# Cross-attention's output projection as seven block products for eight, with weight sums made in DRAM, and two idle products

## The chip, the core and the metric

The kernel runs on one core of a Trainium2 chip. That core has a matrix engine (TensorE; PE in the profile, its weight loads PEld), a vector engine (VectorE, DVE), an activation engine (ScalarE, ACT), GpSimd (POOL) and SyncE (SP), which here only issues DMAs. The metric is the device time of one execution in microseconds (us).

## The reference

One encoder layer on 512 tokens of width 1024 in float32. A state-space branch and a gated MLP branch are merged into the residual `h`; then come cross-attention to 256 memory tokens, a SwiGLU feed-forward layer and a last norm. The change is at the end of the attention, and reaches into the feed-forward layer:

```python
def memory_cross_attention(hn, memn, w_q, w_k, w_v, w_o):
    ...
    p = jax.nn.softmax(s, axis=-1).astype(v.dtype)
    o = jnp.einsum('bhlm,bmhd->blhd', p, v).reshape(bsz, seq, D_MODEL)
    return o @ w_o

def swiglu(hn, w_gate, w_up, w_down):
    return (jax.nn.silu(hn @ w_gate) * (hn @ w_up)) @ w_down
...
        h = h + memory_cross_attention(rms_norm(h, xattn_norm_g[i]), memn,
                                       w_q[i], w_k[i], w_v[i], w_xo[i])
        h = h + swiglu(rms_norm(h, ffn_norm_g[i]), w_gate[i], w_up[i], w_down[i])
```

There are 4 heads of 256; `w_xo` (the reference's `w_o`) is 1024 x 1024; the feed-forward width is 2816.

## The kernel before

**Precision.** Every large product is made of three passes. Each float32 operand is split into a rounded part and a remainder: `split` (L83) casts on ScalarE (L85) and subtracts on VectorE (L86), and `mm3` (L350; L1276 for the block products of the queries and the feed-forward units) multiplies high by high, high by low and low by high into one PSUM bank. So each piece of weights of 128 x 1024 elements a partition block costs a DMA, a cast and a subtract before TensorE may use it. The pieces are listed in a plan in the order of their use. `next_w` (L322) takes the next; it issues the load of the piece three entries ahead (some loads of the feed-forward units 4, 5 or 7 ahead) and the split of the piece two entries ahead. There are three buffers for raw pieces and three for split ones. PSUM has five banks called `mm` and three called `aux`.

**Seven for eight.** The queries (`w_q`), the gate and up weights of the feed-forward layer and `w_down` already use a scheme in which a product of 2 x 2 blocks by 2 x 2 blocks takes seven block products instead of eight, on sums of blocks. Token sums are made by VectorE. Weight sums of `w_q` and `w_down` are made in DRAM: a job copies a block to a scratch tensor by a DMA on SP's queue (L267), and a later DMA on POOL's queue adds another block to it (L268). `plan_sums` (L252) hangs these jobs at given plan entries: (entry of the copy, entries from there to the accumulate). There are 32 jobs: 8 for `w_q`, 24 for `w_down` (`qsum`, `dsum`). The units of gate and up make their weight sums with a POOL DMA and VectorE.

**The stage of the change.** The queries end at about 508 us. Then, head by head, `scores` (L1225) makes softmax probabilities, `turn_probs` transposes them on TensorE and splits them, and `values` (L1259) multiplies them by the values, into `po`, which is split at once into `ot_hi` and `ot_lo`, the transposed attention output. `w_xo` is a plain product: output columns 0 to 511 for all four token tiles by `tokm` (L1364), with the values of heads 1 to 3 called between its pieces, then columns 512 to 1023 (L1376), two token tiles at a time. Each finished bank is added to `h` (L1153), its squares are summed (L475), and when a token's row is complete `norm_feat` scales it (L501), transposes it on TensorE (`to_feat`, L509) and splits it into `fn_hi`, `fn_lo`, which the feed-forward layer reads. That layer begins with 256 leftover columns of gate and up (`pf`), and then takes ten units of 512 columns, seven block products of 24 matmuls each (`px`, `pv`, `pq`); `w_down` follows in seven products (`dx`, `dq`, `dv`), with 42 pieces.

**Order.** The program is written in one order and a scheduler, which goes by its own estimate of the times, may exchange instructions that don't depend on each other, on each engine; what is marked with `in_order` stays. `later(n, f)` puts off the writing of a step by n units of product work. In units 1 and 2 `between` (L1522) puts idle work on TensorE, kept in order, that nobody reads: 15 transposes of 128 columns (`t`, L1527) and two products of 512 columns (`p`, L1529).

## Time and profile before

| | us |
|---|---|
| median of three runs (908.34 to 910.14) | 908.49 |
| the profiled execution | 908.83 |
| its span, first instruction to last | 907.0 |
| queries, values, w_xo: last product of `w_xo` begins | 574.7 |
| feed-forward units end, only `w_down` left | 799.6 |

The page of the profile gives each engine's busy time over the span, then the chain of work that ended last, followed back from the end; its shares say where the time went. Windows give busy time by stage. A group of instructions is listed by its source line, engine, operation and tile names, with its busy time, the mean duration of one in ns, and the idle time ahead of it with what ended it. A mean duration holds a part that overlaps with the next instruction; the distance between starts of instructions that stand back to back, or a chain piece's time divided by its count, is what one more costs. In the chain, `pt` is w_xo (and other token products), `po` values, `psc` scores, `ptr` transposes after a norm.

### The profile page before, as it was taken

The numbers are of one execution on the slowest core, as the hardware profiler recorded it, in microseconds if no ns is written. First come the engines' busy times: TensorE is split into PE (matmuls) and PEld (weight loads), VectorE is DVE, ScalarE is ACT, GpSimd is POOL, SyncE is SP. The second block draws the span as 40 slices with busy tenths as digits, with TensorE's granted clock in tenths as the row PEclk, the third lists the DMA queues.
The fourth block names the chain that finished last, engine by engine and source line by source line (L and its number), as shares of the span: only waits on it lengthen the run. The fifth ranks groups of instructions, "written<-read, shape, count | busy, mean of one in ns | idle before, by whom it ended". The sixth has DMA issues, their size and how long they took to land.

```text
span 907.0 us, 14526 instructions
## 1 busy us (share of the span) xinstructions
PE 895.5 (99%) x5659; PEld 791.6 (87%) x5659; DVE 623.5 (69%) x1018; ACT 475.6 (52%) x696; POOL 104.3 (12%) x165
## 2 busy tenths in 40 slices
PE   9999999999999999999999999999999999999996
PEld 6878888888888887889999978999999999988885
DVE  5696662888753235858956836786778777799875
ACT  5543985144375244446655635655455455565664
POOL 1004320110025301011001001100011100000010
PEclk9999999999999999999999999999999999999999
DMA  7566574586546577863569416527678984246672
GB/s 238 172 161 178 125 179 138 164 201 156 141 135 153 130 198 225 279 190 119 173 221 278 138 51 186 154 58 185 163 198 222 221 198 116 70 139 198 199 234 101
DMA packets 111718, 153.80 MB, mean 170 GB/s; under 512 B 13521, under 2 KB 78561, under 8 KB 111586
## 3 DMA queue, kind: packets, MB, share of 16 engines
q1 hardware_dynamic: 92450, 127.22, 44.4%
q0 software_dynamic: 16608, 24.62, 16.7%
q10 hardware_dynamic: 2592, 1.05, 0.5%
q8 instruction: 44, 0.72, 0.3%
q14 instruction: 24, 0.20, 0.1%
HBM read 146.08 MB, written 38.24 MB: 203 GB/s over the span
## 4 chain that ended last, share of the span: by engine, by line
PE 92%; ACT 3%; DMA 2%; issue 1%; DVE 1%; POOL 0%; SPq 0%; POOLq 0%; DVEq 0%; ACTq 0%
PE pf L350 28%; PE pt L350 16%; PE px L1276 12%; PE dx L350 6%; PE pq L1276 6%; PE dq L350 3%; PE pv L1276 3%; PE qx L1276 2%; PE dv L350 2%; PE pk L789 2%; PE ptr L509 1%; PE psc L350 1%; PE qq L1276 1%; PE po L350 1%; DMA xt<-in_x_dram 1%
## 5 line engine op out<-in xcount | busy, mean ns | idle before, releaser
L86 DVE TENSOR_TENSOR wlo<-wraw,whi 128x1024 fp32r<-128x1024 f32 (+1 forms) x139 | 165.1, 1188 | 109.2 <-ACT whi L85 107.6
L85 ACT CAST whi<-wraw 128x1024 fp32r<-128x1024 f32 (+1 forms) x139 | 142.5, 1025 | 163.1 <-PE pf L350 70.5
L350 PE MATMUL pf<-xn,whi 128*128 128x512 f32 x448 | 140.0, 392 | 0.0
L350 PEld LDWEIGHTS pf<-xn,whi 128*128 128x128 f32 x448 | 83.5, 188 | 17.0 <-issue 0.2
L350 PE MATMUL pf<-xn,wlo 128*128 128x512 f32 x224 | 87.4, 390 | 0.0
L1276 PE MATMUL px<-fn,whi 128*128 128x256 f32 x480 | 84.4, 278 | 0.0
L1276 PEld LDWEIGHTS px<-fn,whi 128*128 128x128 f32 x480 | 72.8, 188 | 0.2
L85 ACT CAST whi<-b 128x1024 fp32r<-128x1024 f32 x40 | 42.2, 1054 | 54.5 <-PE px L1276 29.2
L86 DVE TENSOR_TENSOR wlo<-b,whi 128x1024 fp32r<-128x1024 f32 x40 | 48.9, 1223 | 31.4 <-ACT whi L85 31.4
L1276 PE MATMUL px<-fn,wlo 128*128 128x256 f32 x240 | 66.7, 278 | 0.0
L1276 PE MATMUL pq<-s,whi 128*128 128x256 f32 x320 | 55.7, 278 | 0.0
L350 PE MATMUL dx<-whi,s 128*128 128x512 f32 x170 | 53.6, 391 | 0.4 <-DVE h L1632 0.4
L86 DVE TENSOR_TENSOR wlo<-t,whi 128x1024 fp32r<-128x1024 f32 x30 | 36.7, 1224 | 19.9 <-ACT whi L85 19.9
L85 ACT CAST whi<-t 128x1024 fp32r<-128x1024 f32 x30 | 31.6, 1053 | 35.6 <-PE pv L1276 12.6
L350 PEld LDWEIGHTS pf<-xn,wlo 128*128 128x128 f32 x224 | 42.1, 188 | 8.7
L1276 PEld LDWEIGHTS pq<-s,whi 128*128 128x128 f32 x320 | 48.4, 188 | 0.0
L1276 PEld LDWEIGHTS px<-fn,wlo 128*128 128x128 f32 x240 | 45.2, 188 | 0.0
L1276 PE MATMUL pq<-s,wlo 128*128 128x256 f32 x160 | 44.4, 277 | 0.0
L350 PE MATMUL pt<-whi,xn 128*128 128x512 f32 x128 | 43.6, 412 | 0.1
L350 PEld LDWEIGHTS dx<-whi,s 128*128 128x128 f32 x170 | 31.8, 188 | 7.3 <-issue 0.8
L350 PE MATMUL dx<-wlo,s 128*128 128x512 f32 x85 | 33.1, 391 | 0.0
L1276 PEld LDWEIGHTS pq<-s,wlo 128*128 128x128 f32 x160 | 30.1, 188 | 0.0
(420 smaller groups left out, 2239.2 us busy)
## 6 DMA issues: line engine op xcount, KB each, us to landing
wraw<-in_w_in_dram SPq DMA_DIRECT2D x36, 512.0 KB, 4.3
dsum<-in_w_down_dram SPq DMA_DIRECT2D x20, 512.0 KB, 6.2
wraw<-dsum SPq DMA_DIRECT2D x20, 512.0 KB, 4.4
b<-in_w_gate_dram SPq DMA_DIRECT2D x15, 512.0 KB, 4.7
b<-in_w_up_dram SPq DMA_DIRECT2D x15, 512.0 KB, 4.5
wraw<-in_w_down_dram SPq DMA_DIRECT2D x15, 512.0 KB, 3.6
dsum<-in_w_down_dram POOLq DMA_DIRECT2D x10, 512.0 KB, 7.1
dsum<-dsum POOLq DMA_DIRECT2D x10, 512.0 KB, 6.6
```

The costliest lines, as they stand in the source:

```text
L85: hi = nc.scalar.copy(dst_hi, src)
L86: lo = nc.vector.tensor_tensor(dst_lo, src, dst_hi.bitcast(F32), ALU.subtract)
L350: m = nc.tensor.matmul(ps, a[x], b[y], start=start and i == 0, stop=stop and i == 2, skip_group_check=free)
L509: nc.tensor.transpose(ps[:, j, :], src[:, k * P:(k + 1) * P], ident)
L789: nc.tensor.matmul(ps[32 * j:32 * j + 32, q, :], bd[i][:, g].rearrange("p d c -> p (d c)"), lc(es[i], g), start=(i == 0), stop=False, tile ...
L1276: nc.tensor.matmul(ps[:, j, :], a[x], b[y], start=start and j == k == i == 0, stop=k == 3 and i == 2, skip_group_check=True)
```

## The change

`w_xo` becomes one 2 x 2 block product. Tokens are halved into T0 (0 to 255) and T1, its 1024 rows into K0 and K1 (heads 0 and 1, heads 2 and 3), its columns into two halves. With O the attention output and W the weights, in blocks of 512 rows and columns, the seven products are

| product | token operand | weights | added to h (tokens, columns) |
|---|---|---|---|
| 1 | O(T1,K0) | W00 | + (T1, 0); goes on into 6 |
| 7 | O(T1,K0) - O(T0,K0) | W01 + W11 | - (T0, 1); goes on into 4 |
| 6 | O(T0,K0) - O(T0,K1) - O(T1,K0) | W00 + W01 + W11 | 1 + 6: - (T0, 1), + (T0, 0), - (T1, 1) |
| 5 | O(T0,K0) - O(T0,K1) | W00 + W01 | + (T0, 1); goes on into 3 |
| 4 | O(T0,K1) | W00 + W01 + W11 + W10 | 7 + 4: + (T0, 0) |
| 2 | O(T1,K1) | W10 | + (T1, 0) |
| 3 | O(T1,K1) + operand of 6 | W11 | 5 + 3: + (T1, 1) |

Each has two pieces of weights (c = 0, 1; 12 matmuls of 512 columns each), 14 for eight before. The four weight sums are made in DRAM by eight jobs, put between those of `w_q` and those of `w_down`; the jobs' places in the plan are given anew, so that eight more of the `w_down` jobs come in the feed-forward units. `values` no longer splits `po`; it copies it to `of`, and `attention_part` makes the operands: products 1 and 7 from heads 0 and 1 alone, the others when heads 2 and 3 are there. The first pieces of 1 and 7 stand between the values of heads 1, 2 and 3. Operands 5 and 6 lie in two tiles of the attention's pool. The norms of T0 are begun after product 4, those of T1 after product 3, which is done token tile by token tile. The idle work in units 1 and 2 goes; there are two idle products of 512 columns instead, one after the second product of unit 0 and one after its product 5 (`between()`), reading `fn_hi[:, 4, :]`, where those before read `fn_hi[:, 0, :]`.

```diff
--- before.py
+++ after.py
@@ -220,6 +220,28 @@
 
             plan.append(((w_q, 512 * n, q), [(LOADS, load)], lambda got=got: halves(got.pop("raw"))))
 
+    XSRC = {1: (0, 0), 2: (1, 0), 3: (1, 1)}
+    xsum = {q: dp.tile([P, KD // 2, 512], F32, name=f"xsum{q}") for q in (4, 5, 6, 7)}
+    XO = ((1, 0), (7, 0), (1, 1), (7, 1), (6, 0), (5, 0), (6, 1), (5, 1), (4, 0), (4, 1), (2, 0), (2, 1), (3, 0), (3, 1))
+
+    def xo_block(i, j, c):
+        return block(w_xo, 4 * i + 2 * c, 2, 512 * j, 512)
+
+    def xo_sum(q, c):
+        return xsum[q][:, 2 * c:2 * c + 2, :]
+
+    def plan_xo():
+        for q, c in XO:
+            got = {}
+
+            def load(q=q, c=c, got=got):
+                got["raw"] = wp.tile([P, 2, 512], F32, tag="raw", name="wraw", bufs=3)
+                nc.sync.dma_start(got["raw"], xo_block(*XSRC[q], c) if q in XSRC else xo_sum(q, c))
+
+            plan.append(((w_xo, q, c), [(LOADS, load)], lambda got=got: halves(got.pop("raw"))))
+
     def plan_units(units, down):
 
@@ -258,6 +280,10 @@
             for n in range(2):
                 jobs.append((qsum[q, n], qsum[q + (-1 if q == 6 else 2), n] if first is None else query_block(*first, n),
                              more(n)))
+        for q, first, more in ((5, (0, 0), lambda c: xo_block(0, 1, c)), (7, (0, 1), lambda c: xo_block(1, 1, c)),
+                               (6, (1, 1), lambda c: xo_sum(5, c)), (4, (1, 0), lambda c: xo_sum(6, c))):
+            for c in range(2):
+                jobs.append((xo_sum(q, c), xo_block(*first, c), more(c)))
         for q, i, jc, more in ((5, 0, 0, lambda c: down_block(0, 1, c)), (7, 0, 1, lambda c: down_block(1, 1, c)),
                                (6, 1, 1, lambda c: down_sum(5, c)), (4, 1, 0, lambda c: down_sum(6, c))):
             for c in range(CHUNKS):
@@ -306,9 +332,7 @@
     for half in range(2):
         plan_tok(w_v, half * 512, KD)
     plan_queries()
-    plan_tok(w_xo, 0, KD)
-    for i in range(4):
-        plan_block(w_xo, 2 * i, 2, 512, 512, place=(None, None, 2, 4)[i])
+    plan_xo()
     FS = 2560
     UNITS = [(w, c0) for c0 in range(0, FS, 512) for w in (w_gate, w_up)]
     down_tokens, down_plan = [], []
@@ -316,7 +340,7 @@
     plan_units(UNITS, down_plan)
 
     plan_sums([(5 + 3 * i, 3) for i in range(12)] + [(40 + 2 * i, 2) for i in range(8)] +
-              [(79 + 3 * i, 3) for i in range(3)] + [(116 + 5 * i, 4) for i in range(9)])
+              [(79 + 3 * i, 3) for i in range(3)] + [(122 + 4 * i, 3) for i in range(17)])
     used_w = [0]
 
     def next_w(*key):
@@ -1262,7 +1286,8 @@
             cs = slice(hd * XD + dt_ * P, hd * XD + dt_ * P + P)
             for mt in range(NM):
                 mm3(ps, (vts[0][:, mt, cs], vts[1][:, mt, cs]), (p_hi[:, mt, :], p_lo[:, mt, :]), mt == 0, mt == NM - 1)
-            split(ot_hi[:, 2 * hd + dt_, :], ot_lo[:, 2 * hd + dt_, :], ps)
+            nc.scalar.copy(of[:, 2 * hd + dt_, :], ps)
+        attention_part(hd)
 
     def product(ps, u, q, start, ops):
 
@@ -1342,26 +1367,82 @@
     query_part(3, T0, u2)
     ot_hi = slot("D", (P, KD, T), F32R, "ot_hi")
     ot_lo = slot("E", (P, KD, T), F32R, "ot_lo")
+
+    of = slot("B", (P, KD, T), F32, "of")
+    ot_q = lambda ks, ts: (ot_hi[:, ks, ts], ot_lo[:, ks, ts])
+    xops = {1: ot_q(K0, T1), 2: ot_q(K1, T1), 4: ot_q(K1, T0), 7: ot_q(K0, T0), 3: ot_q(K0, T1)}
+
+    def attention_part(hd):
+
+        u = slice(2 * (hd % 2), 2 * (hd % 2) + 2)
+        lw = slice(u.start + 4, u.stop + 4)
+        a11, a12, a21, a22 = (of[:, k, t] for t in (T1, T0) for k in (u, lw))
+
+        def operand(q, src):
+            split(xops[q][0][:, u], xops[q][1][:, u], src)
+
+        if hd < 2:
+            operand(1, a11)
+            s3_ = np_.tile([P, 2, 256], F32, tag="ev", name="s3", bufs=2)
+            nc.vector.tensor_tensor(s3_, a11, a21, ALU.subtract)
+            operand(7, s3_)
+            return
+        nc.vector.tensor_tensor(a21, a21, a22, ALU.subtract)
+        nc.vector.tensor_tensor(a11, a21, a11, ALU.subtract)
+        operand(6, a11)
+        operand(5, a21)
+        operand(4, a22)
+        operand(2, a12)
+        nc.vector.tensor_tensor(a12, a12, a11, ALU.add)
+        later(2, lambda: operand(3, a12))
+
+    g_f = gain(ffn_norm_g[0], "g_f")
+
+    def xo_product(ps, q, c, start, stop, w=None, ts=(0, 1)):
+        hi, lo = w or next_w(w_xo, q, c)
+        a = xops[q]
+        for t in ts:
+            tsl = slice(t * P, (t + 1) * P)
+            for k in range(2):
+                mm3(ps[t], (a[0][:, 2 * c + k, tsl], a[1][:, 2 * c + k, tsl]), (hi[:, k, :], lo[:, k, :]),
+                    start and k == 0, stop and k == 1, True)
+        tick(1.35 * len(ts))
+
+    def onto(ps, t0, half, op):
+        for t in range(2):
+            hs = h[:, t0 + t, HALF[half]]
+            nc.vector.tensor_tensor(hs, hs, ps[t], op)
+
+    def half_done(t, half):
+        sum_sq(hss[:, 1, t, half:half + 1], h[:, t, HALF[half]])
+
     values(0, *pts.pop(0))
     probs2 = scores(2)
     probs3 = scores(3)
+    for q, nm in ((5, "kt_hi"), (6, "kt_lo")):
+        s_ = ap_.tile([P, KD, M], F32R, name=nm).rearrange("p (i k) t -> p i k t", i=2)
+        xops[q] = s_[:, 0], s_[:, 1]
     turn(1, probs1)
-
-    def second():
-        values(1, *pts.pop(1))
-        turn(2, probs2)
-        turn(3, probs3)
-
-    def last_two():
-        for i in (2, 3):
-            values(i, *pts.pop(i))
-
-    g_f = gain(ffn_norm_g[0], "g_f")
-    ot = (ot_hi, ot_lo)
-    fn_hi, fn_lo = token_slot("fn", APART)
-    fn = (fn_hi, fn_lo)
-
-    tokm(w_xo, 0, ot, KD, add_evac(0, 1, None), hooks={1: second, 2: last_two})
+    ox = [bank("ox0"), bank("ox1")]
+    xo_product(ox, 1, 0, True, False)
+    values(1, *pts.pop(1))
+    turn(2, probs2)
+    oy = [bank("oy0"), aux("oy1")]
+    xo_product(oy, 7, 0, True, False)
+    values(2, *pts.pop(2))
+    turn(3, probs3)
+    xo_product(ox, 1, 1, False, True)
+    onto(ox, 2, 0, ALU.add)
+    values(3, *pts.pop(3))
+    xo_product(oy, 7, 1, False, True)
+    onto(oy, 0, 1, ALU.subtract)
+    oq = [bank("oq0"), bank("oq1")]
+    xo_product(ox, 6, 0, False, False)
+    xo_product(oq, 5, 0, True, False)
+    xo_product(ox, 6, 1, False, True)
+    onto(ox, 0, 1, ALU.subtract)
+    xo_product(oq, 5, 1, False, True)
     at.close()
     ff = ExitStack()
     fp = ff.enter_context(tc.tile_pool(name="ffn", bufs=1))
@@ -1369,24 +1450,36 @@
     sx = ExitStack()
     stp[0] = sx.enter_context(tc.tile_pool(name="units", bufs=2))
     full = fp.tile([P, KD, T], F32, tag="full", name="full", bufs=1)
-
-    fin = add_evac(1, 1, feat_norm(g_f, fn_hi, fn_lo, full))
-    held = []
-    for t0 in (0, 2):
-        ps = {t: bank(f"pt{t - t0}") for t in (t0, t0 + 1)}
-        for wi in range(2):
-            if t0 == 0:
-                held.append((wi,) + next_w(w_xo, 2 * wi, 2, 512, 512))
-            for t in ps:
-                tok_block(ps[t], t, held[wi:wi + 1], ot, 2, slice(0, 512), wi == 0, False)
-            tick(2.7)
-        if t0 == 0:
-            held += [(wi,) + next_w(w_xo, 2 * wi, 2, 512, 512) for wi in (2, 3)]
-        for t in ps:
-            tok_block(ps[t], t, held[2:4], ot, 2, slice(0, 512), False, True)
-            fin(t, ps[t])
-            tick(2.7)
+    onto(oq, 0, 1, ALU.add)
+    onto(ox, 0, 0, ALU.add)
+    for t in range(2):
+        half_done(t, 1)
+    onto(ox, 2, 1, ALU.subtract)
+    xo_product(oy, 4, 0, False, False)
+    xo_product(oy, 4, 1, False, True)
+    fn_hi, fn_lo = token_slot("fn", APART)
+    fn = (fn_hi, fn_lo)
+    to_fn = feat_norm(g_f, fn_hi, fn_lo, full)
+    for t in range(2):
+        hs = h[:, t, HALF[0]]
+        nc.vector.tensor_tensor(hs, hs, oy[t], ALU.add)
+        half_done(t, 0)
+        to_fn(t, hss[:, 1, t, :])
+    ov = [bank("ov0"), bank("ov1")]
+    xo_product(ov, 2, 0, True, False)
+    xo_product(ov, 2, 1, False, True)
+    onto(ov, 2, 0, ALU.add)
+    for t in (2, 3):
+        half_done(t, 0)
+
+    ws = [next_w(w_xo, 3, c) for c in range(2)]
+    for t in range(2):
+        for c in range(2):
+            xo_product(oq, 3, c, False, c == 1, ws[c], (t,))
+        hs = h[:, 2 + t, HALF[1]]
+        nc.vector.tensor_tensor(hs, hs, oq[t], ALU.add)
+        half_done(2 + t, 1)
+        to_fn(2 + t, hss[:, 1, 2 + t, :])
 
@@ -1461,10 +1554,15 @@
         feat_block(ps, ws[i], fn, KD, 4, ts, ts is T0)
         tick(2.7)
 
+    def between():
+
+        in_order(nc.tensor.matmul(aux("idle"), ops[1][0][:, 0, 0:P], fn_hi[:, 4, :], start=True, stop=True))
+
     gate_part(0, T0)
     begun = unit_start(UNITS[0])
     gate_part(1, T0)
     unit_second(UNITS[0], begun[1])
+    between()
     for i in range(2):
         gate_part(i, T1)
     for j in range(2):
@@ -1519,29 +1617,17 @@
             rows_product(ps, q, c, next_w(w_down, q, c), (0, 1), slice(0, 512), start and c == 0, c == CHUNKS - 1,
                          chunks[0] == c > 0)
 
-    def between(*what):
-
-        rest_ = aux("idle")
-        for w in what:
-            if w == "t":
-                in_order(nc.tensor.transpose(rest_[:, 0:P], ident, ident))
-            else:
-                in_order(nc.tensor.matmul(rest_, ops[1][0][:, 0, 0:P], fn_hi[:, 0, :], start=True, stop=True))
-
     for i, u in enumerate(UNITS):
         final = i == len(UNITS) - 1
         x, v = begun
         q = unit_bank("pq")
-        if i in (1, 2):
-            between(*"tt")
         product(q, u, 5, True, ops)
         if final:
             last_job.append(u)
             make_tokens(1, 0)
         if i == 0:
             split(*fn_q(K0, T1), s3)
-        if i in (1, 2):
-            between(*"pt"[:i])
+            between()
         product(x, u, 6, False, ops)
         u2 = stp[0].tile([P, 2, 256], F32, tag="u2", name="u2", bufs=2)
         u3 = np_.tile([P, 2, 256], F32, tag="ev", name="u3", bufs=2)
@@ -1551,8 +1637,6 @@
         else:
             dx = [bank(f"dx{t}") for t in range(2)]
             down_product(dx, 1, True, range(1))
-        if i in (1, 2):
-            between(*"tttt"[:i * 2 - 1])
         product(x, u, 7, False, ops)
         nc.scalar.copy(u3, x)
         if i == 0:
@@ -1563,8 +1647,6 @@
             down_product(dx, 1, True, range(1, 2))
         V.tensor_tensor(u3, q, u3, ALU.subtract)
         put(u, 1, T1, u3)
-        if i in (1, 2):
-            between(*("tttt", "tt")[i - 1])
         product(x, u, 4, False, ops)
         put(u, 0, T1, x)
         if u[0] is w_up:
```

## The prediction

> **What bounds the kernel now.** I read the page's busy shares first, then the chain that ended last, then that chain in order of time around the change, the busy time by stage, and the groups of the stage.

> ```profile
> span 907.0 us, 14526 instructions
> PE 895.5 (99%) x5659; PEld 791.6 (87%) x5659; DVE 623.5 (69%) x1018; ACT 475.6 (52%) x696; POOL 104.3 (12%) x165
> ...
> PE 92%; ACT 3%; DMA 2%; issue 1%; DVE 1%; POOL 0%; SPq 0%; POOLq 0%; DVEq 0%; ACTq 0%
> ```

> TensorE is the bound: 92% of the chain. A product that goes away is time won, unless something else then comes late. The chain in order of time shows what one product costs:

> ```profile
> 547.75 17.32 PE pt L350 x76
> ...
> 588.18 16.96 PE pf L350 x144
> ...
> 622.11 2.83 PE pq L1276 x24
> 624.93 0.22 PE idle L1527 x2
> 625.15 2.83 PE pq L1276 x24
> 627.98 0.23 PE idle L1529
> 628.21 5.45 PE px L1276 x48
> ...
> 648.54 0.11 PE idle L1527
> 648.64 5.66 PE px L1276 x48
> ...
> 676.85 2.72 PE pv L1276 x24
> ...
> 824.19 14.96 PE dv L350 x66
> ```

> A product of 512 columns costs 14.96/66 = 0.2267 us (the w_xo stretch: 17.32/76 = 0.228). One of 256 columns has two paces: 24 cost 2.83 us or 2.72 us, each kept over long stretches, at the same granted clock (1.00, below), and changing where idle products stand. Next, the stages (us, then busy us of PE, PEld, DVE, ACT, POOL, granted clock, DMA share, GB/s):

> ```profile
> 463.90:508.40 44.50, 44.50 (x394) 44.46 (x393) 28.92 (x42) 26.38 (x43) 2.48 (x3) 1.00 0.81 238
> 508.40:575.00 66.60, 65.66 (x331) 54.14 (x331) 40.22 (x75) 32.62 (x68) 3.02 (x4) 1.00 0.38 111
> 680.00:745.00 65.00, 65.00 (x576) 65.00 (x575) 52.37 (x53) 33.84 (x42) 9.69 (x9) 1.00 0.91 216
> 748.00:780.00 32.00, 32.00 (x285) 32.00 (x284) 24.53 (x25) 16.72 (x21) 1.34 (x1) 1.00 0.34 83
> ```

> The attention values and w_xo are the second line: VectorE is busy 60% of it, PE idle 0.94 us. The feed-forward units are the last two; while sums of w_down are made, DMA is at 0.91. The groups of the second line's window give the durations:

> ```profile
> L86 DVE TENSOR_TENSOR wlo<-wraw,whi 128x1024 fp32r<-128x1024 f32 x5 | 6.1, 1223 | 7.2 <-ACT whi L85 7.2
> L86 DVE TENSOR_TENSOR ot_lo<-po,ot_hi 128x512 fp32r<-128x512 f32 x8 | 5.4, 687 | 11.5 <-ACT ot_hi L85 11.5
> L1153 DVE TENSOR_TENSOR h<-h,pt 128x512 f32<-128x512 f32 x7 | 4.6, 681 | 1.7 <-PE pt L350 1.7
> ```

> **The change part by part.** The sum is made against the profiled execution: 908.83 us, its span of 907.0 and 1.83 around it. It lies 0.34 us (0.04%) above the median of 908.49; 0.2%, 1.8 us, is about what a measurement here can tell from no change.

> Products. Before, w_xo is 4 token tiles x 2 halves x 8 blocks of k x 3 passes = 192 products of 512 columns; after, seven of 2 x 4 x 3 = 168. 24 x 0.2267 = **-5.44 us**, on the path. [...]

> VectorE and the waits it makes in this stage. Added: 14 weight pieces for 8, +6 splits; 14 operand splits for 8, +6 subtracts of 512 columns; 8 sums of tokens; 18 additions to h for 8, +10. Back to back, the timeline has two 1024 splits in 2.36 us and three h additions in 1.88, so 1.18 and 0.63 each: 6 x 1.18 + 24 x 0.63 = 22.2 us. VectorE goes from 40.2 to 62.4 us in a stage that TensorE alone would do in 66.6 - 5.4 = 61.2. It is full. The surplus is 1.2 us. Where a pass depends on it: after each of the last two heads stands copy 0.59, two sums 1.37, cast 0.59, subtract 0.69 = 3.2 us ahead of products 6 and 5. Cover is 36 products x 0.227 = 8.2 us, if the queue ahead of it on VectorE is short. If that cover is gone for both heads, 6.4 us; if there is no new wait and the old 0.94 us goes too, -0.9. I take the surplus plus one wait as long as the longest there now (0.68): **+1.9 us**, near the low end, because VectorE's overfull time can slide past the last product: the sums for tokens 256 to 511 aren't needed until four blocks of 24 products (11 us) later.

> ACT: 6 more casts at 1.05 and 14 of 0.59 (the eight old ones become plain copies): 32.6 + 14.6 = 47 of 61 us, hidden under TensorE. Onto h: product 6 waits until product 1's bank has been added to h, 4 likewise for 7, 3 for 5; one to six pieces of 2.7 us lie between. These are priced in the 6.4. The banks held longer leave two for the transposes of the norm, as many as a tile uses: 0, and at most one 0.35 us group four times over if it does not.

> Idle products. Removed: 15 transposes and two products of 512, in the chain 0.22 + 0.23 + 0.11 + 0.44 + 0.22 + 0.23 + 0.11 + 0.33 + 0.22 = 2.11 us; added: two of 0.23. **-1.65 us**, on the path.

> Pace. Of 78 blocks of 24 products of 256 columns between 575 and 800 us, about 27 go at 2.83 now (the chain: 18 before 628, 2 at 639.7, 4 from 648.6 to 660, 3 after 788). All fast is 27 x 0.11 = -3.0; all slow (78 - 27) x 0.11 = +5.6. The one place where a lone product of 512 columns stands between slow products is 627.98: fast after it. At 648.30 a transpose follows it and the pace is slow. The new ones stand alone, after some four blocks, so I take fast from there, and keep four early and three late slow blocks: 20 x 0.11 = **-2.2 us**.

> DMAs. Eight sums (a copy of 512 KB on SP, an accumulate on POOL) take the places of eight w_down sums early on: same sizes, same places, 0. Their bounds are 0 and, if a weight piece is late by the copy's median 6.2 us once, +6.2; I take 0 since the copies stay as they are. Those eight move into the units: 17 jobs, one per 4 plan entries with 3 between copy and accumulate, for nine at 5 and 4. In the w_xo stage 14 loads come for 8, at a share of 0.38: hidden. Queues: SP issues 14 more (0.37 and 0.56 us each), POOL 8 more (0.87 each), both mostly idle; behind an accumulate that waits for its copy stands the next unit's own accumulate on POOL. Cover for that is three entries (8.2 us) against a copy that lands in 6.2. I take 0, with the upper end in rival D.

> Sum: 908.83 - 5.44 + 1.9 - 1.65 - 2.2 = **901.4 us**, 0.8% below the median.

> **The rivals.**

> B, VectorE becomes the bound: both chains exposed, +6.4 for +1.9: **905.9**. For: 62.4 of 61.2 us. Against: the last w_down stage runs at 72.43 of 84 busy on VectorE with no wait.

> C, the two idle products do not change the pace or set the slow one, and the units go at 2.83 throughout: +5.6 for -2.2: **909.2**, no change. For: at 648.30 and 785.65 slow products follow one of 512. Against: 627.98.

> E, the pace is where it was, because nothing steers it: term 0, **903.6**. [...]

> D, the other side: DMA is the bound in the units. Share 0.34 without jobs, 0.91 with about one per 13.6 us; at one per 10.9 us 0.34 + 0.57 x 1.25 = 1.05, so 5% of 50 entries x 2.72 = 136 us, +6.8; and an accumulate that lands late then holds POOL, another 3 us at each of two or three units with two accumulates in flight (they landed in 10.67 us at worst): 901.4 + 6.8 + 7.5 = **915.7**. It decides once a unit's load takes over four entries, 10.9 us; the slowest now took 9.9. Against: in the first line of the table, jobs at three entries ran beside a load per entry at 238 GB/s, and PE was busy 44.50 of 44.50. [...]

> **How the numbers follow.** Forecast 0.45 (its own range 898.5 to 904), E 0.13, B 0.14, C 0.12, D 0.11; B and C together (about 913.7) 0.05. Faster: forecast, E and B, 0.72; same: C, 0.12; slower: D and B with C, 0.16. The low end is all fast and no new wait, 901.4 - 0.8 - 2.8 = 897.8; the high end takes in C, 909.8. What lies above is 0.16, below some 0.03.

> **What the profile after would show.** Right: 168 products of 512 from w_xo; VectorE over 90% busy from the first of them to the units; the chain there on PE with at most 3 us of idle; units at 2.72 after the second idle product; no wait of a weight cast on a DMA in the units. Wrong: PE waiting for the splits of sums (B), 2.83 through the units (C), PE or ACT waiting on loads of `b` or `t` after 620 us (D).

## The result, and the profile after

Eleven runs of the changed kernel had a median of 905.3 us (903.23 to 908.48), against 909.82 for the kernel before beside them: a ratio of 0.9957, with a 95% interval of 0.9945 to 0.9969. Twelve more runs in another comparison (`e16_changed_again`) had 907.22 against 909.11: 0.9973 (0.9961 to 0.9985). So the change makes the kernel 0.3 to 0.4% faster. The forecast of 901.4 us is 0.9% under 909.82. The sign is right and 905.3 lies inside the outer range (897.8 to 909.8), but above the forecast's own range (898.5 to 904), and the gain is half the forecast or less.

The page of the changed kernel's first profiled execution (908.21 us, near the top of its runs; a second profile, of `e16_changed_again`, was taken of the fastest of its twelve, 903.84 us) begins like this; the last line is the chain's shares by engine.

```profile
span 906.4 us, 14551 instructions
PE 889.8 (98%) x5620; PEld 785.7 (87%) x5620; DVE 643.9 (71%) x1048; ACT 488.1 (54%) x716; POOL 111.0 (12%) x173
...
PE 84%; DMA 4%; ACT 4%; DVE 4%; issue 2%; POOL 0%; SPq 0%; ACTq 0%; POOLq 0%; DVEq 0%
```

TensorE's busy time fell by 5.7 us, the span by 0.6. Its share of the chain went from 92% to 84%: where it left TensorE, it now runs through VectorE, ScalarE and DMAs. The windows say where (us, then busy us of PE, PEld, DVE, ACT, POOL, granted clock of TensorE as a share of full speed, DMA share, GB/s): values and `w_xo`; the first products of the feed-forward layer; all from there to the product `dv` of `w_down`.

```profile
511.40:573.10 61.70, 59.66 (x303) 49.41 (x302) 56.16 (x96) 41.48 (x80) 2.42 (x3) 1.00 0.47 146
573.10:593.10 20.00, 18.41 (x142) 18.09 (x143) 14.32 (x23) 13.87 (x24) 2.38 (x3) 0.91 0.74 209
593.10:822.20 229.10, 229.10 (x1887) 223.66 (x1886) 183.60 (x185) 123.06 (x149) 26.11 (x25) 1.00 0.76 195
```

VectorE is busy 91% of the first window. In the second TensorE is idle for 1.6 us, and its granted clock is 0.91. In the third nothing waits. To compare kernels I cut every trace at the same places: the front (to the first product of the values), the stage (values, `w_xo`, the start of unit 0, until 120 products of the leftover columns are still to come), the units (to the first product of `dv`) and the rest. In us, with the difference to the kernel before:

| | front | stage | units | rest | span |
|---|---|---|---|---|---|
| before | 508.4 | 82.4 | 233.2 | 83.0 | 907.0 |
| predicted | 0 | -3.3 | -4.1 | 0 | -7.4 |
| changed, first profile | +3.0 | -0.8 | -4.0 | +1.2 | -0.6 |
| changed, second profile | +0.8 | -2.6 | -4.0 | +0.8 | -5.0 |
| best version, below | -0.1 | -4.9 | -3.9 | +1.6 | -7.3 |

The units came out as predicted. The stage fell short by 0.7 to 2.5 us, and the front, put at nothing, cost 0.8 or more.

TensorE's waits between 555 and 600 us in the first profile (engine, line, what it waited for: us in total, times, longest):

```profile
PE ptr L533 <- ACT full L537: 1.6, 1, 1.6
PE oq L374 <- DVE wlo L86: 1.5, 2, 1.1
PE pf L374 <- ACT fn L85: 0.6, 1, 0.6
```

None of them is a wait for the operands of products 5 and 6, where the prediction had looked. They stand at product 3 (`oq`), at the norm's transposes (`ptr`) and at the first leftover products (`pf`). The chain in order of time (start, us, what) shows what is behind them:

```profile
555.72 6.29 DMA wraw<-in_w_xo_dram
562.11 1.06 ACT whi L85
563.19 1.23 DVE wlo L86
...
564.83 0.57 POOL r L510
...
568.76 1.15 DVE wlo L86
569.93 3.72 DMA wraw<-in_w_gate_dram
573.67 1.04 ACT s L85
...
575.91 4.24 PE pf L374 x22
```

VectorE did six additions to `h` from 550.89 on, and only then the remainder of a weight piece that had been cast since 552.1. So one of the three raw buffers came free late, at 555.7; the load of product 3's first piece landed at 562.0; ScalarE's cast waited 3.3 us for it. Behind that cast stood the squares of T0's norm, and behind the subtract (563.19) VectorE's part of the norm, whose input `h` had been ready since 560.3. The same thing happens once more with a gate piece (569.93). The last line is a second cost: 22 products of 256 columns in 4.24 us, near half the pace (the granted clock was 0.50 there, see the end of the experiments).

### The profile page after: what moved, and what is told of

Its sections match the earlier page's. It is cut to its first block, busy times and chain, and to the rows that moved or that the text cites. A ratio compares the mean times of both kernels' runs of the same rounds, so it can differ in the third digit from the quotient of the medians.

```text
span 906.4 us, 14551 instructions
## 1 busy us (share of the span) xinstructions
PE 889.8 (98%) x5620; PEld 785.7 (87%) x5620; DVE 643.9 (71%) x1048; ACT 488.1 (54%) x716; POOL 111.0 (12%) x173
## 3 DMA queue, kind: packets, MB, share of 16 engines
q10 hardware_dynamic: 2592, 1.05, 0.5%
## 4 chain that ended last, share of the span: by engine, by line
PE 84%; DMA 4%; ACT 4%; DVE 4%; issue 2%; POOL 0%; SPq 0%; ACTq 0%; POOLq 0%; DVEq 0%
PE pf L374 27%; PE px L1301 12%; PE pt L374 11%; PE dx L374 6%; PE pq L1301 6%; PE pv L1301 3%; PE qx L1301 2%; PE dq L374 2%; PE pk L813 2%; PE po L374 1%; PE psc L374 1%; PE qq L1301 1%; PE ptr L533 1%; DVE wlo L86 1%; PE dv L374 1%
## 5 line engine op out<-in xcount | busy, mean ns | idle before, releaser
L86 DVE TENSOR_TENSOR wlo<-wraw,whi 128x1024 fp32r<-128x1024 f32 (+1 forms) x147 | 174.7, 1189 | 106.3 <-ACT whi L85 104.4
L85 ACT CAST whi<-wraw 128x1024 fp32r<-128x1024 f32 (+1 forms) x147 | 150.6, 1025 | 171.7 <-PE pf L374 67.4
L85 ACT CAST whi<-b 128x1024 fp32r<-128x1024 f32 x40 | 42.1, 1054 | 49.2 <-PE px L1301 26.0
L86 DVE TENSOR_TENSOR wlo<-b,whi 128x1024 fp32r<-128x1024 f32 x40 | 48.8, 1223 | 26.2 <-ACT whi L85 26.2
L85 ACT CAST whi<-t 128x1024 fp32r<-128x1024 f32 x30 | 31.6, 1054 | 31.8 <-PE pv L1301 10.9
L86 DVE TENSOR_TENSOR wlo<-t,whi 128x1024 fp32r<-128x1024 f32 x30 | 36.7, 1225 | 16.5 <-ACT whi L85 16.5
L294 POOL DMA_DIRECT2D dsum<-in_w_down_dram x12 | 13.9, 1158 | 133.9 <-DMA dsum<-in_w_down_dram 130.1
```

Of the source, the lines that this page charges most:

```text
L85: hi = nc.scalar.copy(dst_hi, src)
L86: lo = nc.vector.tensor_tensor(dst_lo, src, dst_hi.bitcast(F32), ALU.subtract)
L294: plan[j + step][1].append((0, lambda d=dst, x=more: nc.gpsimd.dma_start(d, x, accum_op=ALU.add)))
```

## The experiments

**The units: what sets the pace.** The first kernel has the unit part of the change alone.

```diff
 # the kernel before; between(...) gone from units 1 and 2
+    unit_second(UNITS[0], begun[1]); between()
...
+            split(*fn_q(K0, T1), s3); between()
```

> The kernel before, with only the idle products of the feed-forward changed: its 15 transposes and two products of 512 are gone, two single products of 512 stand where the changed kernel has them. Theory (the two terms of the unit part are independent of w_xo: -1.65 for the idle products, -2.2 for the pace): 3.9 us under the kernel before, units from 588 to 800 at 2.72 a block but for a few. Rival (nothing there steers the pace): -1.65 only, with some 27 blocks still at 2.83. Rival (the long row of idle products kept the pace fast later on): all blocks slow, +3.9 us.

Measured: 906.41 us against 909.11 (0.9963, 0.995 to 0.9976). The units took 229.2 us, 4.0 less; the pace went from 2.83 to 2.72 us a block right after the first lone product, at 590 us. The span fell by 2.4, because its front lost 1.4 in the profiled execution: 1.6 us at 33 to 39 us, where the granted clock was 0.73 (the kernel before: 1.00); see the end of the experiments. Note the size: 0.9963 for the two idle products in place of the seventeen, with the old `w_xo`, is not to be told from the whole change (0.9957 and 0.9973). As built, seven block products for eight add nothing that can be shown in the total; the versions with the norm ahead, below, do. The kernel before without any idle product:

> The kernel before without any idle product in the feed-forward. With the two single products alone it was 2.7 us faster than before, its pace going from 2.83 to 2.72 right at the first of them. Theory (the old row of transposes and products flips the pace to and fro, and the lone product of 512 after slow blocks sets the fast one): without any of them the units stay at 2.83, some 78 blocks, slower than before by 5.6 - 2.1 = 3.5 us. Rival (the pace is fast unless something throws it off): fast from some point on, 2 to 4 us faster than before.

Measured: 913.42 us (1.0042, 1.0029 to 1.0054). Every block up to 789 us took 2.83; its chain has, where `e1` has 16.34 us after the lone product,

```profile
588.31 16.96 PE pf L350 x144
```

So without a break there the pace stayed as it was, and the lone product was worth some 7 us. Then one single break at 605 us, of one kind or the other:

```diff
 # the kernel before without idle products
             split(*fn_q(K0, T1), s3)
+            between()    # e14: one product of 512 columns; e15: one transpose
```

> The kernel before without its 17 idle products, but with one product of 512 columns after product 5 of the first unit's high tokens (about 605 us). Without it every block to 800 us took 2.83 us and the kernel 913.4. Theory (a lone product of 512 that waits for nothing sets the fast pace): slow until it, fast from it to the products with w_down: some 64 blocks x 0.11 = 7 us less, 906.5 us. Rival (the flip depends on chance or on the place): still slow, 913 us, or runs of both kinds.

> The same with one transpose of 128 columns in place of the product of 512. Theory (any break in the stream, of whatever length, sets the pace anew): fast after it, 906.5 us. Rival (only a product of 512 sets the fast pace; transposes leave it or flip it back, as at 639 us and 648 us in the kernel before): slow, 913 us.

Measured: 906.16 us (0.9975, 0.9965 to 0.9984) and 906.46 us (0.9973, 0.9964 to 0.9982). Both flip it. The chain of the first:

```profile
605.04 2.83 PE pq L1276 x24
607.87 0.23 PE idle L1466
...
616.28 2.72 PE pv L1276 x24
```

A transpose did as well, so it need not be a product of 512. Next, the changed kernel without its idle products, and with the old seventeen:

```diff
-    between()     # e2: both calls gone
+        if i in (1, 2): between(*"tt")     # e12: and the old four rows back
```

> The changed kernel without its two idle products. My theory of the prediction (a lone product of 512 sets the fast pace): without them the units run at 2.83, 78 blocks by 0.11 = up to +8 us over the changed kernel. Rival (the trace of the changed kernel was at the fast pace at 589 us, before the first of them; they steer nothing): 0.46 us under the changed kernel, their own time.

> The changed kernel with the old 17 idle products in the place of the two: the w_xo part alone. If the parts are independent, it is 2.7 us over the changed kernel (what the idle products alone gained), about 908 us, 1 us under the kernel before: the old row of idle products flips a fast pace to the slow one at the second and third unit. If the pace, already fast before them, is not touched: 1.65 us over the changed kernel, their own time.

Measured: `e2` 905.53 us (0.996, 0.9944 to 0.9976; runs from 902.9 to 909.14), in its profile at 2.72 from 574 us on. `e12`, which is the `w_xo` part alone, 912.88 us: slower than the kernel before (1.0041, 1.0024 to 1.0058) and 5.7 to 7.6 us over the changed one. Its chain shows the old rows of transposes in the new kernel:

```profile
605.75 2.72 PE pq L1301 x24
...
633.47 0.11 PE idle L1620
633.58 2.83 PE px L1301 x24
...
648.41 0.11 PE idle L1620
648.52 5.66 PE px L1301 x48
```

The pace was already 2.72, and a transpose between 2.72 blocks turned it to 2.83; from 660 to 800 us, after the last of the row, every block took 2.83, where in the kernel before the same row ends at 2.72. So in these traces a break does not by itself make the pace fast: after one it was 2.72 or 2.83, and it held until the next break. What at a break decides it was not found. A lone idle product of 512 that waited for nothing was followed by 2.72 in every trace that has one; of those that waited 0.3 us for `fn`, the one in `e3` below was followed by 2.83, those in `e7`, `e8`, `e10` and `e13` by 2.72.

**The stage: amount of work, or order.** First VectorE is relieved: `e3` makes no remainder of `w_xo`, which is then missing from its result. Then one late load is taken away.

```diff
-            plan.append(((w_xo, q, c), [(LOADS, load)], lambda got=got: halves(got.pop("raw"))))
+            hi = ...; nc.scalar.copy(hi, raw); return hi, hi       # e3: no remainder of w_xo
...
+                got["raw"] = np_.tile(..., name="wown") if (q, c) == (3, 0) else wp.tile(...)   # e5
```

> The changed kernel, but the 14 w_xo pieces are not split: the high part stands for both, so the low part of w_xo is left out of the result; every product is still run. VectorE loses 14 subtracts of 1.2 us = 17 us in the stage, and a raw buffer comes free after ACT's cast. Theory (what the stage lost went to a raw buffer that VectorE freed late, with the load of the next-to-last product's piece, the norm and the split of fn behind it): the load of that piece is issued some 3 us sooner, PE has no wait over 0.3 us between 573 and 590 and stays at full clock there: about 3.9 us under the changed kernel. Rival (the stage lost it to DMA traffic, not to VectorE): within 1 us of the changed kernel. Rival (the slow time lies in the stages ahead, +3 us before 467 us): also within 1 us.

> The changed kernel, but the first piece of product 3 is loaded into a buffer of its own, so that its load does not wait until VectorE has freed one of the three; VectorE has all its work. Theory (late load, then the norm stands behind that piece on ACT and VectorE): ACT no longer waits 3.3 us for it, the T0 norm starts about 3 us sooner, PE's waits of 1.6 and 1.5 us after product 3 shrink below 0.5 together and the half clock after them goes: 3 to 4 us under the changed kernel. Rival (VectorE is simply full: 22 us more work in a stage of 61): the waits come back in another place, within 1 us of the changed kernel.

Measured: `e3` 903.94 us (0.9941, 0.9929 to 0.9953), 1.4 to 3.3 under the changed kernel's two medians, for 17 us less work on VectorE; a wait of 1.9 us for `fn` and the half pace were still there. `e5` 910.33 us (1.0015, 1.0006 to 1.0025), 3 to 5 us **slower** than the changed kernel: my theory of one late load fell. The piece was there in time (cast at 558.5), but the second piece now had the late buffer, and subtracts of the unit's weights moved ahead of the norm in VectorE's queue; the norm's last scaling on VectorE came at 571.5, not 567.4, and TensorE waited 2.6 us for it, 1.7 and 1.4 for what follows: 5.7 us, against 3.7 in both profiles of the changed kernel. Not all of the loss is in these waits. The granted clock was halved for 6.8 us at this place (573.5 to 580.3 us; for 3.4 in the changed kernel's first profile, not at all in its second), and its mean over an execution was 0.993 in the profiled one, 0.990 to 0.994 in the eleven runs, against 0.993 to 0.999 in the 23 of the changed kernel. So one load was not the cause. `e3` takes away work on VectorE and pieces from the queue at once, so it does not tell amount from order. To test the order alone, the norm was put ahead by force:

```diff
+            def make(q=q, got=got):
+                pinned[0] = q == 3          # cast and subtract of product 3's pieces
+                hl = halves(got.pop("raw")) # stay behind what was written before them:
+                pinned[0] = False           # squares and scaling of T0's norm
+                return hl
```

> The changed kernel, all its work and loads, but the casts and subtracts of the two pieces of product 3 are pinned behind the squares and the scaling of the first two token tiles' norm on ScalarE and VectorE, so that the norm does not stand behind a piece whose load is late. Theory (what the stage lost is the ORDER in VectorE's and ScalarE's queues: the norm that the feed-forward waits for stands behind late pieces): the scaling for those tiles starts some 3 us sooner, PE waits about 1 us for the first piece of product 3 and under 0.5 us more until the unit's second product is through; no half clock; 2 to 3.5 us under the changed kernel. Rival (VectorE is full, whatever the order, as when the first piece got a buffer of its own and the waits only moved): the waits move to product 3 or to the unit's weights, sum of waits between 560 and 592 unchanged (3 to 4 us), within 1 us of the changed kernel or slower.

Measured: 903.48 us (0.9935, 0.9922 to 0.9949), 1.8 and 3.7 under the changed kernel's medians, with all its work and all its loads. (The profiled execution, 901.85, is the fastest of its five.) VectorE in the profile (start, us, engine, line, operation):

```profile
558.59 0.16 DVE L514 TENSOR_TENSOR ms<-hss 128x1 f32<-128x1 f32 x1 [0.26 <-ACT sq L505]
559.68 1.42 DVE L531 SCALAR_TENSOR_TENSOR xs<-h,r,g_f 128x512 f32<-128x512 f32 x2
...
562.94 1.22 DVE L86 TENSOR_TENSOR wlo<-wraw,whi 128x1024 fp32r<-128x1024 f32 x1
564.08 0.68 DVE L1421 TENSOR_TENSOR h<-h,ov 128x512 f32<-128x512 f32 x1
```

The scaling begins at 559.7, where it was 565.4 (563.4 on this front), and the piece of product 3 comes after it; TensorE waits 0.8 us for that, and 1.0 in three more places. The stage is 4.0 us under the kernel before, 1.4 better than the changed kernel's second profile, which had no halved clock in it either (1.00 from 570.5 to 589), and 3.2 better than its first. There is no half pace. So the order is shown to matter with the amount of work unchanged.

**The sums in DRAM.** In the rest, TensorE waited 0.2 to 1.2 us for weight remainders at `dv`, while the last sums were under way (to 827 us).

```diff
-              [(79 + 3 * i, 3) for i in range(3)] + [(122 + 4 * i, 3) for i in range(17)])
+              [(59 + 4 * i, 3) for i in range(4)] + [(79 + 3 * i, 3) for i in range(3)] + [(122 + 4 * i, 3) for i in range(13)])
```

> The changed kernel, with four of its 17 late sums of w_down moved ahead to the stage of w_k and w_v, so that none is still under way when the products with w_down begin. Theory (the sums that run beyond 800 us make the raw loads of w_down late, the waits of dv for wlo are theirs): the 0.5 to 2.0 us of waits at the start of dv go, 0.5 to 1.5 us under the changed kernel. Rival (VectorE's order there makes them): unchanged, within 0.5 us. Rival (four more sums beside the w_k and w_v stage make loads late there): that stage longer, slower by up to 2 us.

> Both of the two edits before: norm ahead of product 3's pieces, four sums sooner. If both theories hold the gains add: 3 to 5 us under the changed kernel, about 901 us. If VectorE is full whatever the order: no more than 1 us under it.

Measured: 906.74 us (0.9974, 0.9964 to 0.9985) and 904.72 us (0.9943, 0.9931 to 0.9956). Neither can be told from the same kernel with the sums late (0.9957 and 0.9973; 0.9935): no gain. The wait at `dv` was gone, as the first theory says. But the front was 3.5 and 4.6 us longer than before, 2.7 and 1.8 of it among the queries: in `e6`, `qv` waited 1.3 us at 470 and the blocks after this break took 2.83 until 504; in `e8` it waited 0.6. And the wait at `dv` is no mark of the late sums: it was absent with them in `e7`, and in `e15`, the kernel before but for its idle products, the rest was 1.5 us longer. It comes and goes.

The other loss, 0.5 to 1.5 us at 336 to 347 us, was in every profile so far of a kernel with sums of `w_xo`, and in none of a kernel without. TensorE waits there for `ya_hi` or `yg_hi`, whose input is read back from DRAM, for 1.1 us in the second profile and 0.6 before. Two other orders of the early sums, both with the norm ahead:

```diff
+        jobs[12:20] = jobs[16:20] + jobs[12:16]                                # e10
...
+        xo, dn = jobs[12:16], jobs[16:]                                        # e13
+        jobs[12:] = [dn[0], dn[5], dn[1], dn[2]] + xo + dn[3:5] + dn[6:]
```

> The kernel with the norm ahead, and the order of the early sums changed: the last four sums of w_xo change places with four of w_down, so that at 329 to 347 us, where two sums run beside the reads of the scan's result, sums of w_down stand as in the kernel before. Theory (the sums of w_xo cost more DMA time there than those of w_down in the same places, copy 10.5 to 11.0 us against 8.0, accumulate 10.1 against 7.6, and PE waits 0.5 to 1.0 us more for ya_hi and yg_hi): those waits go back to 0.6 us, the first product of w_q starts 0.9 us sooner; 0.5 to 1 us under the kernel with the norm ahead alone. Rival (chance of the run): no difference.

> The kernel with the norm ahead, with another order of the early sums: at 329 us stands the sum of w_down's sixth chunk, which is 256 KB and not 512, as in the kernel before; sums of w_xo and of w_down of 512 KB alike had cost 0.5 to 1.0 us of waits for ya_hi there. Theory (what the stage at 336 to 347 us lost is the size of that one sum: 256 KB before, 512 after): copy lands in about 3.1 us and its accumulate in 7.6, PE's wait for ya_hi is 0.6 us again, first product of w_q 0.9 us sooner; 0.5 to 1 us under the kernel with the norm ahead, about 902.6 us. Rival (other traffic): the waits stay at 1 us or more.

Measured: `e10` 903.12 us (0.9939), the same as `e7`; its front was still 0.9 us longer there. Sums of `w_down` are no cheaper than those of `w_xo`. But the sum that stood at 329 us before was that of `w_down`'s sixth chunk, with one row block for two. The DMA lists from 300 us to 352 us, before and after:

```profile
dsum<-in_w_down_dram SPq DMA_DIRECT2D x1, 256.0 KB, 3.1
```

```profile
xsum<-in_w_xo_dram SPq DMA_DIRECT2D x1, 512.0 KB, 3.9
```

With that half sum back in its place, `e13` had 901.54 us (900.79 to 901.9): 0.9918 of the kernel before, 0.9906 to 0.9931. The copy landed in 3.2 us, the wait was 0.6 again, the front 0.06 us shorter than before. This is the fastest kernel found; it is 1.6 and 1.9 us under `e10` and `e7`, of which the half sum explains the 1.0 us that `e7`'s front was longer. The rest is not explained, and with four runs not clear of noise. Last, `e10` without its two idle products:

```diff
-    between()          # both calls
```

> The same without the two idle products, the fastest version that the runs so far point to. Theory (the pace is set anew at breaks in TensorE's stream, such as the transposes and waits around 585 us, and was fast there in the kernel with the norm ahead before its first idle product): fast from 585 us on, 0.5 us and the idle's own wait of 0.3 us less: about 0.8 us under the one before, 902 us or less. Rival (the idle products hold the pace): slow, up to 8 us over it.

Measured: 907.55 us, twelve runs from 900.86 to 912.34, five of them under 903 and seven over 906. The profiled one, at 908.4, took 2.83 for all blocks from 581 us on; its chain has

```profile
583.07 16.96 PE pf L381 x144
```

The gap between the two groups of runs fits one pace or the other throughout; of the faster group no profile was taken. The idle products earn their 0.5 us: without them the pace seems left to chance.

**The changed kernel once more.**

> The changed kernel itself once more, for a second profile. Theory (0.5 to 1.0 us of its 3.0 us in front of w_q come from the sum at 329 us and belong to the kernel, 1.6 us at 39 us and the half clock after 575 us come and go from run to run): the waits of 1.3 to 1.9 us around 566 to 575 us are there again, the first product of w_q comes at 465 or 466.5 us.

Measured: 907.22 us (903.84 to 908.83); the profiled execution had 903.84. The waits were there (2.1, 1.4 and 0.2 us), the first product of `w_q` came at 464.8. There was no half pace; its chain has for the same 22 products

```profile
573.84 2.51 PE pf L374 x22
```

Both stretches that came and went are the granted clock. Windows of the first profile at 576 us and at 33 us, and of the kernel before at 33 us:

```profile
576.00:579.00 3.00, 3.00 (x15) 3.00 (x16) 2.73 (x4) 2.54 (x6) 0.00 (x0) 0.50 0.05 17
33.30:37.20 3.90, 3.90 (x11) 3.10 (x12) 1.08 (x3) 2.46 (x3) 0.00 (x0) 0.59 0.77 163
```

```profile
33.30:37.20 3.90, 3.90 (x18) 3.21 (x19) 1.66 (x5) 3.33 (x6) 0.00 (x0) 1.00 0.76 195
```

The clock was halved for 3.4 us (twice that in `e5`): some 1.7 us lost after the waits at 566 to 575 (4.24 for 2.51), 1.5 to 1.8 after sixteen products of 32 columns at 31 us. The latter is in 6 of 17 profiles (0.72 to 0.74 from 33.3 to 39.5 us, 1.00 in the other eleven), of kernels with and without the `w_xo` part. The former is in five of the seven profiles that have the stage's long waits (mean granted clock of the whole execution 0.995 in the first profile, 0.996 in `e3`, 0.993 in `e5` and `e12`, 0.992 in `e6`). It is not in the other two, `e2` and `e16` (0.998 and 0.999), nor in `e7` and `e13`, with the norm ahead (0.998 both).

What decides it is not shown. In the first profile the clock changes at 33.06, 36.48, 575.78, 579.20 and 903.46 us; the distances are 1, 158, 1 and 95 times 3.41 us. Here are the 3.41 us just before the halving at 575.78, and as long a stretch with the end of the longest wait in the second profile, where the clock stayed at 1.00:

```profile
572.37:575.78 3.41, 1.26 (x9) 0.86 (x8) 3.41 (x6) 2.10 (x4) 0.00 (x0) 1.00 0.68 208
```

```profile
571.94:575.35 3.41, 2.16 (x19) 2.17 (x20) 3.41 (x6) 3.01 (x5) 0.00 (x0) 1.00 0.12 40
```

TensorE is idle for 2.15 us in the first and for 1.25 in the second, whose wait of 2.1 us began at 571.1. But as long a stretch begun at 570.0 in the second profile has 2.3 us of idle time, more than the first, and nothing was halved after it. So idle time in just any 3.41 us does not decide it. That it counts by stretches with fixed bounds, so that waits of about the same length cost 1.7 us or nothing by where they fall, would fit the distances in the first profile and these two stretches; it is my estimate from them, and no run tested it. At 33 us idle time is not the reason: TensorE is busy for all of the 3.41 us before.

## Why the prediction was right or wrong

Of the 7.4 us forecast, 3.5 to 4.9 are missing, and no single term carries them. The second profile, with a mean granted clock of 0.999, lacks 0.7 us in the stage, 0.8 in the front and 0.8 in the rest. The halved clock, which was in no term, takes up to 1.1 us more on average, by an estimate from the mean granted clock: 0.9958 in the changed kernel's 23 runs, 0.9970 in the 25 of the kernel before beside `e16`, over 907 us. That makes 3.5; what is missing beyond it in the second comparison is not accounted for.

**Products, -5.44: right.** The traces have 168 products of `w_xo` for 192. With the norm ahead and the half sum the stage is 4.9 us shorter, with 0.23 for an idle product in it; 0.3 is left for new waits.

**VectorE and the waits, +1.9: the step that failed.** What was left of -5.44 in the stage makes this term 2.6 (second profile) to 4.4 us (first), inside its bounds of -0.9 to 6.4, of which 1.7 in the first is the halved clock. (In the second the blocks before the first idle product went at 2.72 as well, up to 5 x 0.11 us that the prediction had not counted there, so the term may be that much larger.) The prediction took VectorE's surplus, 1.2, plus one wait of 0.68, and looked at the operands of products 5 and 6. Those had their cover: no wait there. Nor was VectorE overfull: it was busy 56.2 us of 61.7, where the sum had 62.4 of 61.2. And the chain did not stay on TensorE there, as it should have. It did not ask what a nearly full engine does to the order in which small, urgent work is served: it said that the overfull time "can slide past the last product", but the norm of T0 cannot, because the feed-forward layer begins with it. What set the price was the norm's place in a queue: pinned ahead, with all of VectorE's work, the term measured 1.2 in `e7` and 0.3 in `e13`. Less work helps too (`e3`), but is not needed.

**Idle products and pace, -1.65 and -2.2: right in size, half right in reason.** The units gave -4.0 for -4.1. The lone product does set the pace (`e9`, `e14`), but so does a transpose (`e15`), and in the changed kernel the pace was at 2.72 already before the first of them. What the prediction missed is that the two parts are not independent: with the old idle products the `w_xo` part alone is 0.4% slower than the kernel before, and with the new ones alone the old `w_xo` is 0.37% faster.

**DMAs, 0: wrong by about +0.9.** "Same sizes, same places" holds for all but one: 512 KB for 256 KB at 329 us, in front of a read-back that TensorE waits for. `e13` gave it back. The other sum moves cost nothing that could be shown. The rest's +0.8 to +1.2 was in no term; since it comes and goes in kernels of both sorts, no cause is given for it.

**The rivals.** B's 905.9 is close to what was measured, but not for its reason: the chains behind heads 2 and 3 were not exposed. C fell (2.72 in the units up to 780 us). E, that nothing steers the pace, fell with `e9` and `e14`. D fell: the DMA share was 0.93 at 680 to 745 us, and 0.75 where it had been 0.34, and TensorE waited for nothing there.

## What to carry to other kernels

When a change fills a side engine to 90%, do not price its surplus alone: follow each urgent step through that engine's queue and ask which piece with a late load stands ahead of it, then pin the urgent step. Here a gain in one place (an own buffer for one load) only moved the wait. When transfers change places, compare the size of each one in the crowded stretch with the one that stood there, not their number. And when two parts of a change both touch when TensorE's stream breaks, time each alone: here a retuning of idle work gained as much in the old kernel as the whole change did, and the new algorithm with the old idle work was a loss.

## What the hardware did unexpectedly

Twenty-four products of 256 columns take 2.72 or 2.83 us (113 or 118 ns each) at the same granted clock of 1.00. Which it is holds over hundreds of products (2.72 in the kernel before from 663 to 786 us, some 1080 products; 2.83 in `e9` from 588 to 698 us). Where it changed, the stream had been broken: by a transpose of 0.11 us (`e15`, 2.83 to 2.72; `e12`, 2.72 to 2.83), or by a product of 512 columns of 0.23 us (`e14`, 2.83 to 2.72). After a wait of 1.3 us in `e6` it was 2.83.
